# Second mixer of a two-block transformer: a head's output step cut into pieces that stand before later projections' weight loads

## The chip, the cores and the metric

The kernel runs on one core of a Trainium2 chip. The metric is the device time of one execution in microseconds. The times before are 2347.97, 2349.81 and 2349.92 us, median 2349.81 us. A profiled execution of its own stands beside them.

## The reference, cut to what matters

Two transformer blocks over 512 tokens of width 1024, in float32. The first block has a feed-forward part, a mixer of windowed and sparse attention, and a second feed-forward part. The second block has a hybrid mixer and a mixture of 32 experts. The change lies in the hybrid mixer only:

```python
def _hybrid_mixer(u, ...):
    proj = u @ w_in
    gq, gk, gv, gg, gdown, rq, rk, rv, rg, mga, mgb = jnp.split(proj, splits, axis=-1)
    log_a = log_sigmoid(gdown @ gk_up + gk_bias) / 16          # decay, per token and key column
    o_gla = gla(heads(gq * 128 ** -0.5), heads(gk), heads(gv), heads(log_a))       # 4 heads, 128 -> 256
    o_gla = _rmsnorm(o_gla, gla_norm_w) * silu(gg)
    o_ret = retention(rotary(rq), rotary(rk) * 256 ** -0.5, heads(rv))             # 4 heads, 256 -> 512
    o_ret = _group_norm(o_ret, ret_norm_w) * silu(rg)
    y_a, y_b = o_gla @ w_br_gla, o_ret @ w_br_ret
    return (sigmoid(mga) * y_a + sigmoid(mgb) * y_b) @ w_out
```

In the gated linear attention (GLA) a score of query i and key j is a sum over 128 columns of q, k and exp(cum_i - cum_j), where cum is the running sum of the decay. In the retention the score of q and k is multiplied by a fixed power of the distance.

## The kernel before, in words

Activations stand feature-major: a tile is 128 features by 512 tokens. Each float32 matrix product is made of three matmuls with operands split into a high and a low part (`mm3`, lines 99 to 101). For each 512 KB block of weights `load_w` issues one DMA on SP's queue into `wraw` (3 buffers), copies the high part on ScalarE into `whi` (line 84) and takes the low part on VectorE into `wlo` (line 85); `whi` and `wlo` have two buffers each, so that the weights of one projection are split while the one before is multiplied. `gemm` then runs 8 x 3 matmuls of 512 columns.

The second mixer (`mixer2`, line 1000) goes through these steps:

- `gla_decay`: decay sums for all 4 heads.
- GLA, head by head: projections q, k (`gla_qk`) and two gates (`silu_tile`: projection, sigmoid by ScalarE, product on GpSimd); for heads 0 and 2 the values of two heads (`vproj`); then `gla_core`, which builds the 512 x 512 score matrix in ten levels. A level (`level(s)`) makes exp of decay differences and multiplies k and q with them into a tile `gf` (two buffers, VectorE lines 917 and 918); matmuls `gs` follow (lines 927, 933, 950), and their result is split into `sh` and `sl` or put into `sd` by mask. The `gs` matmuls have two PSUM banks. The core is a chain between TensorE and VectorE; matmuls of the next head's projections stand between its steps.
- `head_out`: scores times values (`pvo`, three matmuls a piece), copies `o` and squares `osq` on ScalarE, a sum of the squares on GpSimd (line 816), and then a closure `rest`: a matmul with ones (`on`, line 822), two ScalarE functions for the reciprocal root (`hr_ln`, lines 175 and 177), for each of the head's 2 (GLA) or 4 (retention) tiles a GpSimd product gate * hr (line 826), a VectorE product into `o` (line 828), and its split into `fh` and `fl` (lines 84 and 85).
- After four GLA heads, 8 times: a projection with `wma`, its sigmoid, and the branch product `ya` of the 8 `fh`/`fl` tiles with `wbg`.
- Retention, two heads and then the branch product `yb`, twice: per head two projections each for q and k with rotation (`ret_qk`), `vproj`, four gates, `ret_core` (scores `rs`, then `head_out`). Head 2's q is projected before the first `yb` loop, its k after it. Before the second `yb` loop stand 8 projections with `wmb`.

`rest` is held back: `head_out` stores `[wait, rest]` in `self.pend`, each `proj2` counts one down behind its matmuls (`flush(1)`, line 741), and at zero all of `rest` is issued there. `wait` is 3 for GLA (behind the next head's first gate) and 1 for retention (behind the next head's first projection). `flush()` without a number issues it at once.

The text of the kernel is not the order of issue. A planner in the compiler lays out each engine's queue beforehand: the position in the text is a priority, and an instruction whose operands are due by the planner's own estimate of durations is taken before one with a higher priority that is not. On the chip each queue is then worked through in that fixed order.

Of the kernel before, what the change touches and what calls it, by code (L numbers as in the profile page):

```python
# [9 lines left out]
F32 = mybir.dt.float32  # L10
# [29 lines left out]
class Kern:  # L40
# [694 lines left out]
        tp.release()  # L735

    def proj2(self, src):
        w = self.load_w(src)
        ps = self.acc("pj2")
        self.gemm(ps, w, self.X, DT)  # L740
        self.flush(1)
        return ps

    def sigma(self, ps, a=None):
# [49 lines left out]

        return (self.m2.tile([128, 4, 512], F32R, name="sh"), self.m2.tile([128, 4, 512], F32R, name="sl"))

    def head_out(self, V, c0, nt, sh, sl, wname, w0, gates, wait):

        nc = self.nc
        vh, vl = V  # L800
        O = []
        ssum = None
        for t in range(nt):
            po = self.ps.tile([128, 512], F32, name="pvo", tag="tp", bufs=2)
            for j in range(4):
                q = slice(128 * j, 512)
                v = slice(c0 + 128 * t, c0 + 128 * t + 128)
                self.mm3(po[:, q], vh[:, j, v], vl[:, j, v], sh[:, j, q], sl[:, j, q], j == 0, j == 3)
            o = self.m2.tile([128, 512], F32, name="o", bufs=4)
            nc.scalar.activation(o, po, AF.Copy)  # L810
            sq = self.m2.tile([128, 512], F32, name="osq", bufs=2)
            nc.scalar.activation(sq, po, AF.Square)
            if ssum is None:
                ssum = sq
            else:
                nc.gpsimd.tensor_tensor(out=ssum, in0=ssum, in1=sq, op=OP.add)
            O.append(o)
        F = self.F

        def rest():  # L820
            p = self.ps.tile([128, 512], F32, name="on", tag="pv", bufs=1)
            nc.tensor.matmul(p, self.ones, ssum, start=True, stop=True)
            r = self.rstd_from(p, 1.0 / (128 * nt), "hr", None)
            for t in range(nt):
                g = gates[t]
                nc.gpsimd.tensor_tensor(out=g, in0=g, in1=r, op=OP.mult)
                o = O[t]
                nc.vector.scalar_tensor_tensor(o, o, self.vcol(wname, w0 + t), g, op0=OP.mult, op1=OP.mult)
                fh = self.m2f.tile([128, 512], F32R, name="fh", bufs=8)
                fl = self.m2f.tile([128, 512], F32R, name="fl", bufs=8)  # L830
                self.split(o, fh, fl)
                F.append((fh, fl))
        self.pend = [wait, rest]
        self.flush(0)

    def flush(self, n=99):

        if self.pend:
            self.pend[0] -= n
            if self.pend[0] <= 0:  # L840
                f, self.pend = self.pend[1], None
                f()

    def gla_decay(self):

# [33 lines left out]
        nc.vector.tensor_tensor(out=k, in0=self.proj2(A["wg"][:, h, 1]), in1=self.rstd, op=OP.mult)  # L879
        return q, k  # L880

    def gla_core(self, h, q, k, V, gates):

        nc = self.nc
        c = self.cum[h]
        tot = lambda b: c[:, b, 127:128]
        sh, sl = self.s_tiles()
        sd = self.m3.tile([128, 4, 128], F32, name="sd", bufs=1)  # L890
# [30 lines left out]
        def put(src, dst):  # L921
            self.split(src, dst(sh), dst(sl))

        f = level(256)
        p = self.ps.tile([128, 512], F32, name="gs", tag="lg", bufs=2)
        for j in range(2):
            nc.tensor.matmul(p[:, j * 256:j * 256 + 256], f[:, j * 128:j * 128 + 128], f[:, 256:512],
                             start=(j == 0), stop=(j == 1), skip_group_check=True)
        put(p.rearrange("p (j i) -> p j i", j=2), lambda t: t[:, 0:2, 256:512])
        f = level(128)  # L930
        p = self.ps.tile([128, 512], F32, name="gs", tag="lg", bufs=2)
        for n, j in enumerate((0, 2)):
            nc.tensor.matmul(p[:, n * 128:n * 128 + 128], f[:, j * 128:j * 128 + 128],
                             f[:, j * 128 + 128:j * 128 + 256], start=(n == 0), stop=(n == 1),
                             skip_group_check=True)
        for n, j in enumerate((0, 2)):
            put(p[:, n * 128:n * 128 + 128], lambda t: t[:, j, j * 128 + 128:j * 128 + 256])
        for n, s in enumerate((64, 32, 16, 8, 4, 2, 1, 0)):
            a = b = level(s) if s else None
            if not s:  # L940
                a, b = k, q
            p = self.ps.tile([128, 512], F32, name="gs", tag="lg", bufs=2)

            t = s or 128
            up = lambda v: v.rearrange("p (m u t) -> p m u t", u=2, t=s)[:, :, 1] if s else \
                v.rearrange("p (m t) -> p m t", t=t)
            w = 64 if s else 128
            for j in range(4):
                x = slice(j * 128, j * 128 + 128)
                nc.tensor.matmul(p[:, j * w:j * w + w].rearrange("p (m t) -> p m t", t=t), a[:, x], up(b[:, x]),  # L950
                                 start=(j == 0), stop=(j == 3), skip_group_check=True)
            m = up(self.gmask[:, n])
            nc.vector.copy_predicated(
                sd.rearrange("p j (m u t) -> p j m u t", u=2, t=s)[:, :, :, 1] if s else sd.unsqueeze(2),
                m.unsqueeze(1).to_broadcast([128, 4] + list(m.shape[1:])),
                p[:, 0:4 * w].rearrange("p (j m t) -> p j m t", j=4, t=t))
        for j in range(4):
            put(sd[:, j], lambda t: t[:, j, j * 128:j * 128 + 128])
        self.head_out(V, 256 * (h % 2), 2, sh, sl, "gla_norm", 0, gates, 3)

    def ret_qk(self, h, which):

# [20 lines left out]

    def ret_core(self, h, Q, K, V, gates):
        nc, A = self.nc, self.A
        dec = self.m3.tile([128, 512], F32, name="dec", bufs=1)
        nc.sync.dma_start(dec, A["decay"][:, h])
        sh, sl = self.s_tiles()
        for j in range(4):
            p = self.ps.tile([128, 512], F32, name="rs", tag="lg", bufs=2)  # L990
            q = slice(128 * j, 512)
            x = slice(128 * j, 128 * j + 128)
            for e in range(2):
                self.mm3(p[:, q], K[e][0][:, x], K[e][1][:, x], Q[e][0][:, q], Q[e][1][:, q], e == 0, e == 1)
            s = self.m3.tile([128, 512], F32, name="rsc", bufs=2)
            nc.vector.tensor_tensor(out=s[:, q], in0=p[:, q], in1=dec[:, 0:512 - 128 * j], op=OP.mult)
            self.split(s[:, q], sh[:, j, q], sl[:, j, q])
        self.head_out(V, 0, 4, sh, sl, "ret_norm", 4 * h, gates, 1)

    def mixer2(self):  # L1000
        nc, A = self.nc, self.A
# [5 lines left out]
        nc.sync.dma_start(self.gmask, A["gmask"])  # L1007
        ma = self.dram.tile([128, DT, 512], F32, name="ma")
        yb = self.dram.tile([128, DT, 512], F32, name="yb")
        self.pend = None  # L1010
        self.gla_decay()
        self.F = []
        V = None
        for h in range(4):
            if h == 0:
                V = self.vproj(A["wgv"][:, h // 2], False)
            q, k = self.gla_qk(h)
            gates = [self.silu_tile(A["wg"][:, h, 2 + t]) for t in range(2)]
            if h == 2:
                V = self.vproj(A["wgv"][:, h // 2], False)  # L1020
            self.gla_core(h, q, k, V, gates)
        for n in range(DT):
            _, s = self.sigma(self.proj2(A["wma"][:, n]))
            self.flush()
            w = self.load_w(A["wbg"][:, n])
            po = self.acc("ya")
            self.gemm(po, w, self.F, DT)
            t = self.m2.tile([128, 512], F32, name="mt", tag="gate", bufs=4)
# [6 lines left out]
        for c in (0, 1):  # L1035
            nc.vector.tensor_tensor(out=self.cs[:, c], in0=self.cs[:, c], in1=self.rstd, op=OP.mult)
        M = []
        Q = None
        for half in range(2):
            F = self.F = []  # L1040
            for h in (2 * half, 2 * half + 1):
                Q = Q or self.ret_qk(h, 0)
                K = self.ret_qk(h, 1)
                V = self.vproj(A["wrv"][:, h], True)
                gates = [self.silu_tile(A["wr"][:, h, 4 + t]) for t in range(4)]
                self.ret_core(h, Q, K, V, gates)
                Q = None
            if half == 0:
                Q = self.ret_qk(2, 0)
            if half == 1:  # L1050
                m3.release()
                sp = self.pool("sig")
# [1 line left out]
                for n in range(DT):  # L1054
                    _, g = self.sigma(self.proj2(A["wmb"][:, n]), sp.tile([128, 512], F32, name=f"sg{n}"))
                    sg.append(g)
            self.flush()
            for n in range(DT):
                w = self.load_w(A["wbr"][:, half, n])
                po = self.acc("yb")  # L1060
                self.gemm(po, w, self.F, DT)
                t = self.m2.tile([128, 512], F32, name="mt", tag="gate", bufs=4)
# [10 lines left out]
                h = self.xp.tile([128, 512], F32R, name=f"oh{n}", tag=f"xh{n}")  # L1073
# [9 lines left out]
        for n in range(DT):  # L1083
            w = self.load_w(A["wo2"][:, n])
# [710 lines left out]
```

## Time and profile before

| | |
|---|---|
| median of three runs | 2349.81 us |
| profiled execution, its own time | 2345.84 us |
| span of its trace | 2344.0 us |
| TensorE busy | 2272.5 us, 97% |
| VectorE busy | 1151.0 us, 49% |
| ScalarE busy | 856.7 us, 37% |
| GpSimd busy | 402.7 us, 17% |
| second mixer, in the trace | about 1020 to 1810 us |

The table is one execution's. Busy TensorE is time with a matmul in flight; a wait of TensorE is read from the view of waits, and a lowered clock from the granted clock of a stretch. In the second mixer a projection of 24 matmuls takes about 5.4 us.

### The profile page before, as it was taken

To read this page: it belongs to the slowest core of one execution; us is meant where nothing else is said; L and a number is where in the kernel's file an instruction comes from. 1 tells how busy PE (TensorE), PEld (TensorE's weight loads), DVE (VectorE), ACT (ScalarE), POOL (GpSimd) and SP (SyncE) were. 2 spreads that over 40 slices of the span, in tenths; PEclk is the share of its full clock that TensorE was granted. 3 is DMA by queue.
4 is the path that set the end of the run, shared out by engine and by line. 5 is a ranking of instruction groups with operands and counts; after the bars stand their busy time and mean duration, and the time that the engine had idled before them with its cause. 6 is when DMAs were issued, how large, how long until landed. Compare 5 with 4: busy or idle time off the path is not lost.

```text
span 2344.0 us, 27722 instructions
## 1 busy us (share of the span) xinstructions
PE 2272.5 (97%) x10344; PEld 1674.3 (71%) x10344; DVE 1151.0 (49%) x2074; ACT 856.7 (37%) x1441; POOL 402.7 (17%) x408
## 2 busy tenths in 40 slices
PE   8999999999999999999999999999999899999997
PEld 6888888776788888877877887787878544444443
DVE  4544445888754444457674445435464333322223
ACT  5322234676642222344444354334553211100012
POOL 1000003335310000014340121203123211111001
PEclk9999999999999999999999999999999899999999
DMA  5533335221133333332213322232247999999997
GB/s 168 172 94 93 104 100 162 84 61 50 45 113 99 91 98 99 117 118 63 72 60 111 106 83 83 88 113 69 89 125 229 363 398 407 406 407 406 406 408 304
DMA packets 126098, 390.83 MB, mean 167 GB/s; under 512 B 15398, under 2 KB 21071, under 8 KB 125704
## 3 DMA queue, kind: packets, MB, share of 16 engines
q1 hardware_dynamic: 121064, 380.10, 47.3%
q10 hardware_dynamic: 2592, 4.72, 0.5%
q0 software_dynamic: 2304, 4.20, 0.5%
q8 instruction: 83, 1.36, 0.2%
q14 instruction: 55, 0.45, 0.1%
HBM read 378.44 MB, written 17.33 MB: 169 GB/s over the span
## 4 chain that ended last, share of the span: by engine, by line
PE 87%; DVE 5%; DMA 3%; ACT 3%; POOL 1%; issue 1%; SPq 0%; POOLq 0%; DVEq 0%; ACTq 0%
PE pg L1339 5%; PE pj L101 5%; PE pj L99 5%; PE pj L100 5%; PE pu L1339 5%; PE po L100 4%; PE po L101 4%; PE po L99 4%; PE pd L1339 4%; PE pu L101 3%; PE pu L99 3%; PE pu L100 3%; PE pg L100 3%; PE pg L101 3%; PE pg L99 3%; PE py L1406 2%
## 5 line engine op out<-in xcount | busy, mean ns | idle before, releaser
L84 ACT ACTIVATE whi<-wraw 128x1024 fp32r<-128x1024 f32 (+2 forms) x290 | 296.2, 1021 | 702.0 <-issue 186.8
L85 DVE TENSOR_TENSOR wlo<-wraw,whi 128x1024 fp32r<-128x1024 f32 (+2 forms) x282 | 347.3, 1232 | 141.2 <-ACT whi L84 135.3
L101 PE MATMUL pj<-xh,wlo 128*128 128x512 f32 x624 | 247.4, 397 | 10.3 <-DVE wlo L85 10.3
L99 PE MATMUL pj<-xh,whi 128*128 128x512 f32 x624 | 250.7, 402 | 0.0
L100 PE MATMUL pj<-xl,whi 128*128 128x512 f32 x624 | 246.1, 394 | 0.0
L157 POOL TENSOR_TENSOR ssq<-ssq,sq 128x512 f32<-128x512 f32 x34 | 53.3, 1566 | 762.4 <-ACT sq L154 761.9
L1339 PE MATMUL pg<-wexp,xs 128*64 128x512 f32 x474 | 163.6, 606 | 2.0 <-DMA wexp<-in_wexp 2.0
L1339 PE MATMUL pu<-wexp,xs 128*64 128x512 f32 x474 | 159.8, 592 | 0.0
L99 PE MATMUL pg<-xh,whi 128*128 128x512 f32 x352 | 139.1, 395 | 6.7 <-ACT xh L142 6.7
L101 PEld LDWEIGHTS pj<-xh,wlo 128*128 128x128 f32 x624 | 118.5, 190 | 36.2 <-DVE wlo L85 12.0
L100 PE MATMUL pg<-xl,whi 128*128 128x512 f32 x352 | 138.4, 393 | 0.5 <-DVE xl L143 0.5
L101 PE MATMUL pg<-xh,wlo 128*128 128x512 f32 x352 | 138.1, 392 | 0.0
L101 PE MATMUL pu<-xh,wlo 128*128 128x512 f32 x352 | 137.1, 389 | 0.4 <-DVE wlo L85 0.4
L100 PE MATMUL po<-hl,whi 128*128 128x512 f32 x352 | 137.1, 389 | 0.0
L99 PE MATMUL pu<-xh,whi 128*128 128x512 f32 x352 | 137.1, 389 | 0.0
L99 PE MATMUL po<-hh,whi 128*128 128x512 f32 x352 | 137.0, 389 | 0.0
L100 PE MATMUL pu<-xl,whi 128*128 128x512 f32 x352 | 136.9, 389 | 0.0
L101 PE MATMUL po<-hh,wlo 128*128 128x512 f32 x352 | 136.9, 389 | 0.0
L99 PEld LDWEIGHTS pj<-xh,whi 128*128 128x128 f32 x624 | 118.8, 190 | 25.4 <-issue 2.6
L100 PEld LDWEIGHTS pj<-xl,whi 128*128 128x128 f32 x624 | 118.5, 190 | 24.5 <-issue 1.7
L1339 PE MATMUL pd<-wexp,hs 128*64 128x512 f32 x484 | 115.7, 599 | 0.0
L1339 PEld LDWEIGHTS pu<-wexp,xs 128*64 128x64 f32 x474 | 49.1, 137 | 77.7 <-issue 77.6
(613 smaller groups left out, 4413.3 us busy)
## 6 DMA issues: line engine op xcount, KB each, us to landing
wexp<-in_wexp SPq DMA_DIRECT2D x358, 512.0 KB
wraw<-in_w1i SPq DMA_DIRECT2D x44, 512.0 KB
wraw<-in_w2i SPq DMA_DIRECT2D x44, 512.0 KB
wraw<-in_wr SPq DMA_DIRECT2D x32, 512.0 KB
wpark<-in_wexp SPq DMA_DIRECT2D x48, 256.0 KB
wraw<-in_wg SPq DMA_DIRECT2D x16, 512.0 KB
wraw<-in_wrv SPq DMA_DIRECT2D x16, 512.0 KB
wraw<-in_wbr SPq DMA_DIRECT2D x16, 512.0 KB
```

Of the source, the lines that this page charges most:

```text
L84: return (self.nc.scalar.activation(hi, src, AF.Copy), (eng or self.nc.vector).tensor_tensor(out=lo, in0=src, in1=hi.bitcast(F32), op=OP.s ...
L85: (eng or self.nc.vector).tensor_tensor(out=lo, in0=src, in1=hi.bitcast(F32), op=OP.subtract))
L99: mm(ps, ah, bh, start=first, stop=False)
L100: mm(ps, ah, bl, start=False, stop=False)
L101: mm(ps, al, bh, start=False, stop=last)
L157: self.nc.gpsimd.tensor_tensor(out=self.ssq, in0=self.ssq, in1=sq, op=OP.add)
L1339: self.pe(self.nc.tensor.matmul(out[r], x[:, r], self.loaded[2 * p + j, c][half], start=first, stop=last))
L1406: self.pe(nc.tensor.matmul(ps, oh[:, i * 128:i * 128 + 128], y[:, hf * 512:hf * 512 + 512], start=(first and j == 0), stop=(j == 1)))
```

## The change

It touches the second mixer alone.

- `flush(n)` now takes a list of steps and issues the first n of them. `proj2` calls `flush(1)` ahead of its `load_w`, not behind its matmuls.
- `rest` is cut: `scale` (the matmul `on`, the reciprocal root, all GpSimd products of gates) and `parts(a)` (the VectorE products, `fh` and `fl` of two tiles). The list is: nothing, `scale`, nothing, `parts(0)`, and for retention `parts(2)`. So `scale` stands before the second projection's weights, `parts(0)` before the fourth's, `parts(2)` before the fifth's, for both kinds of heads; the parameter `wait` is gone.
- In GLA the values of the two highest levels (`level(256)`, `level(128)`) are issued between the two gates' projections; the rest of the core is a closure called after the second gate.
- The k of retention head 2 is projected before the first `yb` loop, right behind its q.

```diff
     def proj2(self, src):
+        self.flush(1)
         w = self.load_w(src)
         ps = self.acc("pj2")
         self.gemm(ps, w, self.X, DT)
-        self.flush(1)
         return ps
...
-        def rest():
+        def scale():
             p = self.ps.tile([128, 512], F32, name="on", tag="pv", bufs=1)
             nc.tensor.matmul(p, self.ones, ssum, start=True, stop=True)
             r = self.rstd_from(p, 1.0 / (128 * nt), "hr", None)
-            for t in range(nt):
-                g = gates[t]
+            for g in gates:
                 nc.gpsimd.tensor_tensor(out=g, in0=g, in1=r, op=OP.mult)
-                o = O[t]
+
+        def parts(a):
+            for t in (a, a + 1):
+                g, o = gates[t], O[t]
                 nc.vector.scalar_tensor_tensor(o, o, self.vcol(wname, w0 + t), g, op0=OP.mult, op1=OP.mult)
...
                 self.split(o, fh, fl)
                 F.append((fh, fl))
-        self.pend = [wait, rest]
-        self.flush(0)
+        wait = [lambda: None]
+        self.pend = wait + [scale] + wait + [lambda a=a: parts(a) for a in range(0, nt, 2)]
 
     def flush(self, n=99):
 
-        if self.pend:
-            self.pend[0] -= n
-            if self.pend[0] <= 0:
-                f, self.pend = self.pend[1], None
-                f()
+        for _ in range(min(n, len(self.pend))):
+            self.pend.pop(0)()
...
-        f = level(256)
...
-        f = level(128)
...
+        f, f2 = level(256), level(128)
+
+        def core(V, gates):
+            nonlocal f
...
+            f = f2
...
+            self.head_out(V, 256 * (h % 2), 2, sh, sl, "gla_norm", 0, gates)
+        return core
...
             q, k = self.gla_qk(h)
-            gates = [self.silu_tile(A["wg"][:, h, 2 + t]) for t in range(2)]
+            gates = [self.silu_tile(A["wg"][:, h, 2])]
+            core = self.gla_core(h, q, k)
+            gates.append(self.silu_tile(A["wg"][:, h, 3]))
             if h == 2:
                 V = self.vproj(A["wgv"][:, h // 2], False)
-            self.gla_core(h, q, k, V, gates)
+            core(V, gates)
...
-                K = self.ret_qk(h, 1)
+                K = K or self.ret_qk(h, 1)
...
-                Q = None
+                Q = K = None
             if half == 0:
-                Q = self.ret_qk(2, 0)
+                Q, K = self.ret_qk(2, 0), self.ret_qk(2, 1)
```

## Rows read from the trace of the kernel before

**Rows 1.** The page's busy time of the engines, with shares of the span.
```profile
PE 2272.5 (97%) x10344; PEld 1674.3 (71%) x10344; DVE 1151.0 (49%) x2074; ACT 856.7 (37%) x1441; POOL 402.7 (17%) x408
```
**Rows 2.** Waits of TensorE, 1040 to 1800 us: who for whom, total us, times, longest.
```profile
PE pj L101 <- DVE wlo L85: 10.3, 3, 3.8
PE gs L950 <- DVE sl L85: 6.7, 2, 3.6
PE ya L99 <- ACT fh L84: 1.8, 1, 1.8
PE yb L100 <- DVE fl L85: 1.5, 2, 1.3
...
PE on L822 <- POOL osq L816: 0.7, 1, 0.7
```
**Rows 3.** Stretches: length, busy PE PEld DVE ACT POOL, granted clock, DMA.
```profile
1104.00:1118.00 14.00, 10.87 (x51) 8.95 (x49) 12.15 (x19) 7.06 (x14) 8.36 (x8) 0.88 0.09 32
1203.00:1217.00 14.00, 10.43 (x50) 8.79 (x49) 11.89 (x18) 7.41 (x14) 8.68 (x8) 0.88 0.11 36
1394.00:1426.00 32.00, 28.20 (x113) 22.41 (x112) 21.26 (x22) 10.22 (x14) 13.17 (x10) 0.89 0.17 50
1478.00:1512.00 34.00, 31.23 (x123) 24.05 (x123) 18.35 (x18) 11.62 (x17) 11.48 (x8) 0.90 0.21 64
1604.00:1640.00 36.00, 32.20 (x141) 26.21 (x141) 21.50 (x22) 12.46 (x18) 16.25 (x11) 0.95 0.16 45
1688.00:1718.00 30.00, 27.28 (x125) 22.30 (x125) 17.00 (x19) 18.23 (x29) 10.25 (x7) 1.00 0.30 88
...
1114.00:1116.00 2.00, 2.00 (x9) 1.75 (x8) 1.26 (x2) 1.59 (x4) 0.85 (x2) 0.50 0.00 0
```
**Rows 4.** Timeline of VectorE, GLA heads 0 to 1: start, us, instruction, count.
```profile
1095.70 1.22 DVE L85 TENSOR_TENSOR wlo<-wraw,whi 128x1024 fp32r<-128x1024 f32 x1
1096.83 0.84 DVE L917 TENSOR_TENSOR gf<-gk,gd__9220 128x256 f32<-128x256 f32 x1
...
1105.33 3.48 DVE L828 SCALAR_TENSOR_TENSOR o<-o,vec,gate 128x512 f32<-128x512 f32 x2
1108.74 1.47 DVE L85 TENSOR_TENSOR fl<-o,fh 128x512 fp32r<-128x512 f32 x2
...
1111.39 0.88 DVE L85 TENSOR_TENSOR sl<-gs,sh 128x512 fp32r<-128x512 f32 x2
```
**Rows 5.** Timelines of GpSimd and of TensorE, the same stretch.
```profile
1094.14 1.30 POOL L816 TENSOR_TENSOR osq<-osq 128x512 f32<-128x512 f32 x1 [3.50 <-ACT osq L812]
...
1103.57 2.99 POOL L826 TENSOR_TENSOR gate<-gate,hr_ln 128x512 f32<-128x512 f32 x2 [3.83 <-ACT hr_ln L177]
...
1099.88 1.02 PE L822 MATMUL on<-osq,ones 128*128 128x512 f32 x2
```
**Rows 6.** Timeline of SP's queue, while the first `ya` product is under way.
```profile
1228.34 0.33 SPq L1034 DMA_DIRECT2D csr<-csd  x1
```
**Rows 7.** Timeline of VectorE, retention heads 0 to 1.
```profile
1402.93 5.17 DVE L828 SCALAR_TENSOR_TENSOR o<-o,vec,gate 128x512 f32<-128x512 f32 x3 [1.19 <-POOL gate L826]
1408.02 1.88 DVE L85 TENSOR_TENSOR fl<-o,fh 128x512 fp32r<-128x512 f32 x3
1409.83 0.74 DVE L828 SCALAR_TENSOR_TENSOR o<-o,vec,gate 128x512 f32<-128x512 f32 x1
1410.49 1.27 DVE L971 TENSOR_TENSOR rt<-pj,csr 128x512 f32<-128x512 f32 x2
1411.69 1.37 DVE L85 TENSOR_TENSOR fl<-o,fh 128x512 fp32r<-128x512 f32 x1
1412.98 2.28 DVE L85 TENSOR_TENSOR wlo<-wraw,whi 128x1024 fp32r<-128x1024 f32 x1
```
**Rows 8.** Timelines of GpSimd and of ScalarE, the same stretch.
```profile
1401.60 5.95 POOL L826 TENSOR_TENSOR gate<-gate,hr_ln 128x512 f32<-128x512 f32 x4 [4.74 <-ACT hr_ln L177]
...
1408.67 1.05 ACT L84 ACTIVATE whi<-wraw 128x1024 fp32r<-128x1024 f32 x1
```

More of the change, by code (lines that the diff above doesn't have):

```diff
@@ L795, in s_tiles, with head_out @@
         return (self.m2.tile([128, 4, 512], F32R, name="sh"), self.m2.tile([128, 4, 512], F32R, name="sl"))
-    def head_out(self, V, c0, nt, sh, sl, wname, w0, gates, wait):
+    def head_out(self, V, c0, nt, sh, sl, wname, w0, gates):
         nc = self.nc
@@ L880, in gla_qk, with gla_core @@
         return q, k
-    def gla_core(self, h, q, k, V, gates):
+    def gla_core(self, h, q, k):
         nc = self.nc
@@ L922, in put @@
             self.split(src, dst(sh), dst(sl))
-        f = level(256)
[L925 to L929, printed above, removed]
-        f = level(128)
-        p = self.ps.tile([128, 512], F32, name="gs", tag="lg", bufs=2)
@@ L932, in gla_core @@
[L932 to L941, printed above, removed]
-            p = self.ps.tile([128, 512], F32, name="gs", tag="lg", bufs=2)
[L944 to L947, printed above, removed]
-            for j in range(4):
[L949 to L956, printed above, removed]
@@ L957, in gla_core @@
-        for j in range(4):
-            put(sd[:, j], lambda t: t[:, j, j * 128:j * 128 + 128])
-        self.head_out(V, 256 * (h % 2), 2, sh, sl, "gla_norm", 0, gates, 3)
+        f, f2 = level(256), level(128)
+        def core(V, gates):
+            nonlocal f
+            p = self.ps.tile([128, 512], F32, name="gs", tag="lg", bufs=2)
+            for j in range(2):
+                nc.tensor.matmul(p[:, j * 256:j * 256 + 256], f[:, j * 128:j * 128 + 128], f[:, 256:512],
+                                 start=(j == 0), stop=(j == 1), skip_group_check=True)
+            put(p.rearrange("p (j i) -> p j i", j=2), lambda t: t[:, 0:2, 256:512])
+            f = f2
+            p = self.ps.tile([128, 512], F32, name="gs", tag="lg", bufs=2)
+            for n, j in enumerate((0, 2)):
+                nc.tensor.matmul(p[:, n * 128:n * 128 + 128], f[:, j * 128:j * 128 + 128],
+                                 f[:, j * 128 + 128:j * 128 + 256], start=(n == 0), stop=(n == 1),
+                                 skip_group_check=True)
+            for n, j in enumerate((0, 2)):
+                put(p[:, n * 128:n * 128 + 128], lambda t: t[:, j, j * 128 + 128:j * 128 + 256])
+            for n, s in enumerate((64, 32, 16, 8, 4, 2, 1, 0)):
+                a = b = level(s) if s else None
+                if not s:
+                    a, b = k, q
+                p = self.ps.tile([128, 512], F32, name="gs", tag="lg", bufs=2)
+                t = s or 128
+                up = lambda v: v.rearrange("p (m u t) -> p m u t", u=2, t=s)[:, :, 1] if s else \
+                    v.rearrange("p (m t) -> p m t", t=t)
+                w = 64 if s else 128
+                for j in range(4):
+                    x = slice(j * 128, j * 128 + 128)
+                    nc.tensor.matmul(p[:, j * w:j * w + w].rearrange("p (m t) -> p m t", t=t), a[:, x], up(b[:, x]),
+                                     start=(j == 0), stop=(j == 3), skip_group_check=True)
+                m = up(self.gmask[:, n])
+                nc.vector.copy_predicated(
+                    sd.rearrange("p j (m u t) -> p j m u t", u=2, t=s)[:, :, :, 1] if s else sd.unsqueeze(2),
+                    m.unsqueeze(1).to_broadcast([128, 4] + list(m.shape[1:])),
+                    p[:, 0:4 * w].rearrange("p (j m t) -> p j m t", j=4, t=t))
+            for j in range(4):
+                put(sd[:, j], lambda t: t[:, j, j * 128:j * 128 + 128])
+            self.head_out(V, 256 * (h % 2), 2, sh, sl, "gla_norm", 0, gates)
@@ L997, in ret_core @@
             self.split(s[:, q], sh[:, j, q], sl[:, j, q])
-        self.head_out(V, 0, 4, sh, sl, "ret_norm", 4 * h, gates, 1)
+        self.head_out(V, 0, 4, sh, sl, "ret_norm", 4 * h, gates)
     def mixer2(self):
@@ L1009, in mixer2 @@
         yb = self.dram.tile([128, DT, 512], F32, name="yb")
-        self.pend = None
+        self.pend = []
         self.gla_decay()
@@ L1046, in mixer2 @@
                 self.ret_core(h, Q, K, V, gates)
-                Q = None
+                Q = K = None
             if half == 0:
-                Q = self.ret_qk(2, 0)
+                Q, K = self.ret_qk(2, 0), self.ret_qk(2, 1)
             if half == 1:
```

## The prediction

> **What bounds the kernel now.** The page comes first: TensorE is busy for 2272.5 us, 97% of the span, and the next, VectorE, for 49% [rows 1]. So a change that adds no matmul and removes none can only win back TensorE's idle time and the time in which it ran slowly. The view of its waits says where that is in the second mixer [rows 2]: 10.3 us in three waits of a projection for the low part of its weights (`wlo`), 6.7 us in two waits of a GLA core for a split score tile (`sl`), 1.8 us of `ya` for `fh`, and waits of `yb` for `fl` and its like. The windows around them give each stall its idle time (length less busy PE) and the clock [rows 3]: idle 3.1, 3.6, 3.8, 2.8, 3.8 and 2.7 us. All six lie just behind the output of a head: A and B at GLA heads 1 and 3, D and F at retention heads 1 and 3, E where `yb` follows head 1, G where the `wmb` projections follow head 3. After five of them TensorE runs for some microseconds at the lower of its two levels, 1.2 GHz (the row with 0.50 shows two of A's). A window's length times (1 - clock) bounds what that costs: 1.7, 1.7, 3.5, 3.4, 1.8 and 0 us. Idle 19.8 and clock 12.1 make 31.9 us, the ceiling.
>
> The timelines say why. In A, VectorE had its two `o` products from 1105.33 to 1108.81 and their `fl` until 1110.2, and only then reached the core's `sl`, which TensorE stood waiting for until 1112.2 [rows 2, 4]. The `o` products came so late because `on` ran at 1099.88, behind the first gate's projection, and the GpSimd products only from 1103.57 [rows 5], though the sum of squares was there at 1095.44 [rows 5]. In D the whole output of four tiles goes through at once: three `o` beside the GpSimd products (5.17 us), `fl`, the fourth `o`, rotation, the last `fl`, and then the fourth projection's `wlo`, which ends at 1415.26 [rows 7]. Its `whi` on ScalarE waited from the same cause, behind the third `fh` [rows 8].
>
> **The change, part by part.** *`scale` earlier in GLA* (3 places: heads 0 to 1, 1 to 2, 2 to 3). `on` no longer has to stand behind k's and the gate's projections; its only condition is the sum, at 1095.44. So it comes 4.4 us earlier (1099.9 - 1095.5), and with it everything behind: the last `fl` ends at 1105.8 in place of 1110.2. The core's first `sl` could then run as soon as its scores are there, and stalls of 3.1 and 3.6 us go, with their 1.7 us of clock each. What is late next is the sum itself: the one `on` that was issued straight behind its sum cost TensorE 0.7 us of waiting [rows 2]; I charge that at all three places. Saved: A 3.1 + 1.7 - 0.7 = 4.1, B 3.6 + 1.7 - 0.7 = 4.6, heads 1 to 2 (no such stall, since `vproj` lies between) -0.7.
>
> *`parts` in two pieces in retention.* `on` keeps its place, behind the first projection. The queues are laid out beforehand and what is due is taken early: the load of `csr`, whose text stands behind eight `ya` products, is issued at 1228.34, during the first [rows 6]. So a piece whose gates are ready is taken when VectorE is free, wherever its text stands, and only what still competes with the rotation and `wlo` at the end gives way. That is the last `o` and its `fl`, 0.74 + 1.37 = 2.1 us [rows 7]. `wlo` ends 2.1 us earlier, and of 3.8 us in D and F 1.7 remain. The bounds are 0 saved (the planner's order stays as it is) and 3.8 (the third tile gives way too, and `whi` with it). I take the middle because the row shows the fourth `o` already separated from the first three. Half of the clock's share is kept as a cost. D: 3.8 + 3.5 - 1.7 - 1.7 = 3.9; F: 3.8 + 1.8 - 1.7 - 0.9 = 3.0; G, the same with a sigmoid in the rotation's place: 2.7 - 0.6 = 2.1.
>
> *Head 2's k before `yb`.* Two more projections (10.8 us) now lie between `on` and the first `yb`; the last `fl` has long been there. E's 2.8 + 3.4 us go. But the boundary now has the form of D, four projections behind a head, and gets D's remainder, 1.7 + 1.7. Saved: 2.7. The projections themselves are moved, with their 512 KB loads on SP's queue, by one loop; their cover does not change, because the next head's values follow directly in both forms.
>
> *Levels 256 and 128 between the gates.* Their `gf` were already made early: one of the four halves stands at 1096.83 in VectorE's queue, ahead of `on` and of the second gate's projection [rows 4, 5], and the `gs` matmuls keep their place behind that projection. Costed at nothing; the gates' projections cover them, and without that cover they are at most 4 x 0.84 = 3.4 us of VectorE per head.
>
> *GpSimd's products moved by 4.4 us in GLA* fall beside a `wlo`. A `wlo` took 1.22 us alone and 2.28 beside GpSimd's rotation [rows 4, 7], and an `o` 0.74 alone against 1.7 beside the gate products [rows 7]. The `wlo` concerned is that of the next head's q, needed only after the second gate's projection, so TensorE does not see the 1.1 us. The Trainium skill, "SBUF — State Buffer", section "Who interferes with whom", speaks against this part: a VectorE instruction with two SBUF inputs and a GpSimd instruction that reads SBUF exclude each other for a whole instruction. The durations agree; were the three `wlo` on the path, that would take 3 x 1.1 = 3.3 us off the sum below, 16.4.
>
> The sum: 4.1 + 4.6 - 0.7 + 3.9 + 3.0 + 2.1 + 2.7 = 19.7 us. The `ya` wait of 1.8 us stays: `flush()` still issues head 3's output whole at that place. The profiled execution took 2345.84 us and would take 2326.1; the median of the runs lies 4.0 higher, so 2349.8 - 19.7 = 2330.1. I say 2330. The experts behind the mixer start their loads from its last loop and shift with it.
>
> **The rivals.** *1: all of it goes.* If the second piece really leaves the queue until it is wanted, D, E, F and G lose all idle and clock. 31.9 less three `on` waits (2.1) is 29.8: 2320. For it: VectorE is under half busy [rows 1]. Against: GpSimd takes 1.49 us per product in a row of four [rows 8], whoever waits for them.
>
> *2: the pieces are taken as early as before.* Then D, F and G stay, and E becomes a second D (3.8 + 3.5 in place of 2.8 + 3.4, 1.1 worse). Only GLA's 8.0 is left: 6.9 us, 2343. For it: rows 6, and a VectorE with nothing else due when the gates come.
>
> *3: slower, the `o` products get ahead of the second gate's weights in GLA.* `parts(0)` now precedes that `load_w` in the text. VectorE works in order: if its queue has the two `o` before that `wlo` (at 1095.70 today, rows 4), `wlo` waits for GpSimd. The pair of `o` would end at 1108.8 - 4.4 = 1104.4, `wlo` at 1105.6, and TensorE wants it at about 1100.8, as the gate's projection begins right behind `on` [rows 5]: 4.8 us of idling and some 2.6 of clock, three times, 22.2 us. With rival 2's retention the whole is 22.2 - 6.9 = 15.3 us slower, 2365; with my terms for retention 2352. It decides once the planner thinks the first gate ready before that `wlo`. On the chip the distance is from 1095.70 to 1095.5 + 3.7 = 1099.2 (from `on` to the gates, rows 5), 3.5 us, which speaks against it.
>
> *4: nothing happens.* The planner lays the same queues, because text position is only a priority: 2349.8.
>
> **How the numbers follow.** My forecast 0.45, rival 1 0.17, rival 2 0.19, rival 3 0.09, rival 4 0.10. The range 2318 to 2348 holds nearly all of the forecast with its bounds, rivals 1 and 2 in the main, and leaves out rival 3 and most of 4. A measurement of this kernel tells about 0.2%, 4.7 us, from no change: faster is below 2345.1 (0.43 + 0.17 + 0.14 from rival 2), slower above 2354.5 (0.06 from rival 3, 0.01 from 4), the rest is the same: 0.74, 0.19, 0.07.
>
> **What would show it.** In the profile after: `on` of GLA heads right behind the sum of squares, and no wait of `gs` for `sl` of 3 us; waits of `pj` for `wlo` shrunk to some 1.7 us each but four of them (D, the new one before `yb`, F, a small G); no wait of `yb` for `fl`; the granted clock at 1.00 around A and B. I am wrong if a new wait of `pj` for `wlo` stands at a GLA head's second gate (rival 3), if D's wait is still 3.8 us (rival 2), or if it is gone (rival 1).

## The result, and the profile after

The kernel after takes 2334.6 us (median of 4 runs, 2332.75 to 2335.86) beside 2349.59 us before on the same chip: ratio 0.994, 95% interval 0.9928 to 0.9952, by the medians 15.0 us less. The forecast was 2330, 19.7 us less.

The two profiled executions differ by 10.0 us only (2345.84 and 2335.86 us): the one of before lay below its median, and in the one of after the unchanged code ahead of the mixer took 2.8 us longer. So two stages are compared inside the traces: "GLA" from the first `pz` matmul (the decay's first) to the last of `ya`, "retention" from the first `rs` to the last of `yb` (starts of matmuls, from the views of these tiles).

| us | before | after | change | forecast |
|---|---|---|---|---|
| GLA | 294.0 | 292.3 | -1.7 | -8.0 |
| retention | 400.6 | 387.8 | -12.8 | -11.7 |
| first `pz` to last `yb` | 760.1 | 745.6 | -14.5 | -19.7 |

So the total hides a miss: retention gave slightly more than its sum, GLA next to nothing.

The page of the kernel after, busy time of the engines (it answers to [rows 1]):

```profile
PE 2266.3 (97%) x10344; PEld 1669.1 (72%) x10344; DVE 1149.6 (49%) x2074; ACT 858.3 (37%) x1441; POOL 400.6 (17%) x408
```

The waits of TensorE in the kernel after, 1020 to 1820 us (they answer to [rows 2]; us in total, times, longest):

```profile
PE pj L101 <- DVE wlo L85: 8.0, 5, 2.6
PE gs L952 <- DVE gf L917: 3.5, 5, 1.5
PE on L822 <- POOL osq L816: 3.3, 4, 1.4
PE ya L99 <- ACT fh L84: 1.8, 1, 1.8
PE vv L100 <- DVE wlo L85: 1.1, 2, 0.5
PE ya L101 <- DVE wlo L85: 0.4, 1, 0.4
PE yb L101 <- DVE wlo L85: 0.3, 1, 0.3
```

The 6.7 us of `gs` for `sl` are gone, and so are the waits of `yb` for `fl` and `fh`. In their place stand waits of `gs` for `gf`, of `on` for the sum and of `pj` for `wlo`. The timeline of TensorE has them one by one (start, us, instruction; in brackets the idle time before it and what ended it):

```profile
1098.25 1.12 PE L822 MATMUL on<-osq,ones 128*128 128x512 f32 x2 [0.64 <-POOL osq L816]
...
1116.27 0.52 PE L952 MATMUL gs<-gf 128*128 128x64 f32 x3 [1.47 <-DVE gf L917]
...
1195.44 0.70 PE L822 MATMUL on<-osq,ones 128*128 128x512 f32 x1 [1.40 <-POOL osq L816]
...
1206.25 0.51 PE L101 MATMUL pj<-xh,wlo 128*128 128x512 f32 x1 [2.61 <-DVE wlo L85]
...
1414.17 0.50 PE L101 MATMUL pj<-xh,wlo 128*128 128x512 f32 x1 [1.50 <-DVE wlo L85]
...
1495.25 0.50 PE L101 MATMUL pj<-xh,wlo 128*128 128x512 f32 x1 [1.49 <-DVE wlo L85]
...
1619.65 0.50 PE L101 MATMUL pj<-xh,wlo 128*128 128x512 f32 x1 [1.50 <-DVE wlo L85]
...
1700.12 0.50 PE L101 MATMUL pj<-xh,wlo 128*128 128x512 f32 x1 [0.86 <-DVE wlo L85]
```

The last four are D, the new boundary ahead of `yb`, F and G: the forecast had 1.7, 1.7, 1.7 and 0.6. The fourth row, at the second gate of GLA head 3, is the wait that rival 3 described. VectorE's timeline shows both (first the GLA gate, then D, which answers to [rows 7]):

```profile
1203.52 1.10 DVE L830 SCALAR_TENSOR_TENSOR o<-o,vec,gate 128x512 f32<-128x512 f32 x1
1204.54 1.66 DVE L85 TENSOR_TENSOR wlo<-wraw,whi 128x1024 fp32r<-128x1024 f32 x1
...
1404.08 5.17 DVE L830 SCALAR_TENSOR_TENSOR o<-o,vec,gate 128x512 f32<-128x512 f32 x3 [1.19 <-POOL gate L825]
1409.18 1.88 DVE L85 TENSOR_TENSOR fl<-o,fh 128x512 fp32r<-128x512 f32 x3
1410.99 1.27 DVE L974 TENSOR_TENSOR rt<-pj,csr 128x512 f32<-128x512 f32 x2
1412.19 1.93 DVE L85 TENSOR_TENSOR wlo<-wraw,whi 128x1024 fp32r<-128x1024 f32 x1
1414.04 1.77 DVE L830 SCALAR_TENSOR_TENSOR o<-o,vec,gate 128x512 f32<-128x512 f32 x1
```

In D exactly the fourth `o` and its `fl` have moved behind `wlo`; the first three stay ahead of it, though the text puts the third behind it. In GLA head 3 an `o` stands ahead of the second gate's `wlo`, which ends at 1206.20, and TensorE starts at 1206.25.

### The profile page after: what moved, and what is told of

It reads as the page before. It is cut to its first block, busy times and chain, and to the rows that moved or that the text cites. A ratio compares the mean times of both kernels' runs of the same rounds, so it can differ in the third digit from the quotient of the medians.

```text
span 2334.1 us, 27726 instructions
## 1 busy us (share of the span) xinstructions
PE 2266.3 (97%) x10344; PEld 1669.1 (72%) x10344; DVE 1149.6 (49%) x2074; ACT 858.3 (37%) x1441; POOL 400.6 (17%) x408
## 4 chain that ended last, share of the span: by engine, by line
PE 84%; DVE 5%; DMA 4%; ACT 3%; POOL 2%; issue 1%; SPq 0%; POOLq 0%; DVEq 0%; ACTq 0%
PE pg L1344 6%; PE pu L1344 5%; PE pj L101 4%; PE pj L100 4%; PE pj L99 4%; PE po L100 4%; PE po L101 4%; PE po L99 4%; PE pd L1344 4%; PE pu L101 3%; PE pu L100 3%; PE pu L99 3%; PE pg L101 3%; PE pg L100 3%; PE pg L99 3%; PE py L1411 2%
```

## The experiments

The first two rows are the result above. The other runs were timed beside the kernel before on the same chip, in four batches (e1 to e4; c1 and e5 to e7; e9, e11 and e12; e13), in which the median of before was 2346.69, 2347.01, 2348.7 and 2348.16 us. "Ret." is the retention stage; the waits are those of TensorE in the GLA stage, from 1020 us on; the last column bounds the time lost there to a lowered clock, first between 1020 and 1040 us, then from 1040 us on, worked out from windows of 10 us as length x (1 - granted clock). The stages, waits and clocks are those of one profiled execution of each run, which for e11 and e12 was its fastest.

| run | us | ratio, 95% interval | GLA | ret. | GLA waits | GLA clock |
|---|---|---|---|---|---|---|
| before | 2349.59 | | 294.0 | 400.6 | 10.0 | 3.4 + 5.1 |
| after | 2334.6 | 0.994 [0.9928, 0.9952] | 292.3 | 387.8 | 11.6 | 3.4 + 0 |
| c1, after again | 2334.14 | 0.9947 [0.9933, 0.996] | 292.9 | 387.8 | 11.1 | 0 + 5.1 |
| e1, GLA half only | 2347.01 | 1.0 [0.9991, 1.0009] | 292.4 | 399.5 | 11.7 | 3.5 + 0 |
| e2, retention half only | 2334.44 | 0.9948 [0.9934, 0.9962] | 294.0 | 387.7 | 10.0 | 3.5 + 5.1 |
| e3, k late | 2338.81 | 0.9966 [0.9952, 0.9979] | 292.4 | 392.6 | 11.6 | 3.4 + 0 |
| e4, levels back | 2338.73 | 0.9966 [0.9952, 0.9979] | 295.7 | 387.7 | 11.8 | 1.7 + 6.8 |
| e5, sum on VectorE | 2335.78 | 0.995 [0.9937, 0.9964] | 294.6 | 387.8 | 10.0 | 3.4 + 5.1 |
| e6, retention pieces behind | 2335.52 | 0.9954 [0.994, 0.9967] | 292.9 | 387.4 | 11.1 | 1.7 + 3.4 |
| e7, GLA pieces behind | 2336.3 | 0.9952 [0.9938, 0.9965] | 295.0 | 387.8 | 10.9 | 3.4 + 5.1 |
| e9, second `fl` on GpSimd | 2340.97 | 0.9966 [0.9952, 0.998] | 292.9 | 394.2 | 11.2 | 1.7 + 3.4 |
| e11, gate product early, on after | 2323.98 | 0.9898 [0.9883, 0.9913] | 290.2 | 378.9 | 11.2 | 0 + 1.7 |
| e12, the same, on before | 2317.74 | 0.9872 [0.9857, 0.9887] | 283.6 | 378.9 | 6.9 | 0 + 0 |
| e13, e11 with GLA's output late | 2320.33 | 0.9883 [0.9864, 0.9902] | 285.7 | 378.9 | 7.8 | 1.7 + 0 |

Take the waits and both parts of the clock off the GLA stage and 275.4 to 277.4 us are left in all fourteen rows. So what differs between the rows is waits and clock, and up to 8.6 us of it is clock, which differs between executions of one program too (after and c1).

### Each half alone: e1 and e2

e1 keeps the GLA half and puts retention's output back to `rest` as it was, head 2's k behind `yb`; e2 is its mirror (`nt == 2` held back behind three projections, the levels back in the core). The diff is e1's.

```diff
+        def whole():
+            scale()
+            for a in range(0, nt, 2):
+                parts(a)
+        if nt == 4:
+            self.behind_mm = [1, whole]
+        else:
+            self.pend = wait + [scale] + wait + [lambda a=a: parts(a) for a in range(0, nt, 2)]
...
-                Q, K = self.ret_qk(2, 0), self.ret_qk(2, 1)
+                Q = self.ret_qk(2, 0)
```

> Only the GLA half of the change: scale and parts as steps ahead of the weight loads and the two levels between the gates for GLA heads; retention heads issue their whole output behind the first projection, and head 2's k stands behind the yb loop, both as before. Theory A (from the stages of the two traces: GLA gave about 2 us, retention 14): 2 to 4 us faster than before, ratio 0.998 to 0.999. Theory B (the split that was predicted: GLA 8.0 us): 2341.6, ratio 0.9966. In the trace both expect the retention stalls of 3.8 us at heads 1 and 3 back, with the clock falling there.

> Only the retention half: steps ahead of the loads for retention heads and head 2's k ahead of yb; GLA heads issue their whole output behind the third projection, and the two levels are back in the core. Theory A: 12 to 15 us faster than before, ratio 0.9936 to 0.9949, nearly the whole of the change. Theory B: 11.7 us, ratio 0.995, and clearly short of the changed kernel. Both expect the two waits of gs for sl of 3.1 and 3.6 us back, with the clock falling behind them.

e1 measured 1.0 [0.9991, 1.0009], so GLA's half is worth nothing within 2.1 us, which refutes theory B (8.0 us) and leaves only the low end of theory A; e2 has the whole gain (0.9948). The GLA waits say why: 10.0 us before, 11.7 in e1. The `sl` waits (6.7) went, and `on` (0.7 to 3.4), `gf` (0.8 to 3.5) and `wlo` (0 to 2.6) took their place.

### Parts of the change undone: e3 and e4

e3 takes head 2's k behind the `yb` loop again; e4 puts the two levels back into the core.

```diff
-                Q, K = self.ret_qk(2, 0), self.ret_qk(2, 1)
+                Q = self.ret_qk(2, 0)
```

```diff
-        f, f2 = level(256), level(128)
...
-            nonlocal f
+            f = level(256)
...
-            f = f2
+            f = level(128)
```

> The changed kernel, but head 2's k is projected behind the first yb loop again. Theory A: the yb stall of before comes back (2.8 us idle and up to 3.4 us of clock) in place of 1.8 us of waits for wlo, so 3 to 4.4 us slower than the changed kernel: 0.995 to 0.996 of before. Rival: the pieces are taken early anyhow, the position of k is worth nothing, and the time is the changed kernel's, 0.994.

> The changed kernel, but levels 256 and 128 are issued in the core, behind the second gate, as before. Theory A: no difference from the changed kernel beyond 1 us (0.994), and the wait of 2.6 us for wlo at GLA head 3's second gate stays, since the o products and the sum of squares stand before that wlo. Rival: the levels' VectorE work is what holds that wlo up; without it the wait shrinks below 1 us and the kernel is 2 us faster than the changed one (0.993).

e3: of retention's 12.8 us, 8.0 remain (400.6 to 392.6); k early is worth the other 4.8, not 2.7. The waits of TensorE in e3, 1380 to 1790 us:

```profile
PE yb L99 <- ACT fh L84: 4.4, 1, 4.4
PE pj L101 <- DVE wlo L85: 3.8, 3, 1.5
```

With the pieces cut and k late, `yb` waits longer than before (4.4 us against 2.8 of idle time at E in [rows 3]), and the granted clock behind that is 0.68 over 10 us. The cut alone makes E worse; k early is what makes it safe.

e4 is 4.3 us slower than e2 of the same batch by the medians; the intervals just overlap, but the five executions of e4 (2337.99 to 2340.26 us) all lie above the five of e2 (2333.75 to 2337.79). It is also 4.6 us slower than c1 of another batch. Neither theory had that: the wait for `wlo` at head 3 went, as the rival said, and the time rose. e4 and e2 differ in the early `scale` and `parts` of GLA alone, so e4 against e2 is that step by itself: a loss of some 4 us, which the early levels make up for. The waits are hardly longer than after (11.8 us), but gathered: `gs` waits 6.4 us for `gf` in three places, the longest 3.1. The clock lost 6.8 us there. In the two traces the way from the first `pz` to the last `yb` differs by 1.7 us only (748.9 and 747.2), so one execution of each doesn't show the whole 4.3. e13, below, has the levels early and GLA's output late, and its stage is within 2.1 us of that of e12, which has both late; 1.7 of these are clock at the start of the stage. So the place of the levels seems to matter only beside the early scale; the runs go no further.

### Other orders of the same work: c1, e5, e6, e7

c1 is the kernel after, run again. e5 makes GLA's sum of squares on VectorE. e6 orders retention's `parts(2)` on VectorE behind the low part of the fourth projection's weights, where the text has it anyhow, so that it can't be taken early; e7 orders GLA's `parts(0)` behind the low part of the second gate's weights, which the text puts it ahead of.

```diff
-                nc.gpsimd.tensor_tensor(out=ssum, in0=ssum, in1=sq, op=OP.add)
+                (nc.vector if nt == 2 else nc.gpsimd).tensor_tensor(out=ssum, in0=ssum, in1=sq, op=OP.add)
```

```diff
+        if self.pend and self.pend[0][0]:
+            self.pend.pop(0)[1](self.last_lo)
...
+                if after is not None:
+                    self.behind(ins, after)
```

> The changed kernel once more, on the same chip as the three above, so that they can be compared with it: 12 to 17 us faster than before, ratio 0.993 to 0.995.

> The changed kernel with the sum of a GLA head's squares on VectorE in place of GpSimd. Theory A: TensorE's 3.3 us of waiting for that sum in front of the matmul with ones are a cost of the early scale step, since the planner takes GpSimd's add for shorter than its 1.3 us; with the sum on VectorE (about 0.7 us) the waits fall below 1 us in all, and the kernel is 2 to 3 us faster than the changed one. Rival: the core behind it is a chain that starts no sooner, the idle time turns up in the waits of gs for gf, and the time is the changed kernel's within 1 us.

> The changed kernel with the second two tiles of a retention head's output ordered behind the low part of the fourth projection's weights on VectorE, by a dependency, so that they can't be taken early. Theory A (the third tile in front of that weight's split, on VectorE and ScalarE, makes the remaining waits of 1.5 us): the waits of pj for wlo at retention heads fall from 5.3 us in all below 1 us, and the kernel is 4 to 5 us faster than the changed one, 0.992 of before. Rival: the work only moves behind, in front of the next weights, whose waits (now 1.1 us at the values, 0.3 at yb) grow by as much; the time stays within 1 us.

> The changed kernel with a GLA head's output products ordered behind the low part of the second gate's weights. This moves instructions at the boundary of GLA heads 2 to 3 alone. Theory A: the wait of 2.6 us for that wlo goes, and with it 2 to 3 us of time. Rival: the products come back into the core's start, the wait of gs for gf behind it grows, and less than 1 us is left.

None of them is faster than c1. In e5 the waits for the sum fall from 3.3 us to 0.6, and the longest wait for `gf` rises from 1.5 to 2.8; all GLA waits together are 10.0 us, 1.1 less than c1's, and the time is not. In e7 the 2.6 us at the second gate of head 3 are gone; its waits, 1020 to 1820 us, have them here:

```profile
PE gs L960 <- DVE gf L925: 5.7, 5, 2.8
```

In e6 the retention waits for `wlo` of `pj` fall from 5.3 us to 1.1. Its waits, 1380 to 1790 us:

```profile
PE vv L100 <- DVE wlo L85: 3.6, 2, 1.8
PE yb L101 <- DVE wlo L85: 1.6, 1, 1.6
PE pj L101 <- DVE wlo L85: 1.1, 4, 0.3
```

That is 6.3 us beside 6.7 after. So the rivals had the mechanism in all three: where one wait goes, the next one grows, and the sum of a stage's waits falls by at most 1.1 us beside c1. (The medians lie 1.4 to 2.2 us above c1's, which the intervals don't tell from no difference.) That suggests that TensorE waits less for a place in the queue than for the amount of VectorE's and GpSimd's work between a head's last scores and the next thing that TensorE needs. It is not shown in general: k early and, below, e13 against e11 change nothing but the order, and their stages are 4.8 and 4.5 us shorter.

### Less work for VectorE: e9

The last two tiles' `fl` go to GpSimd.

```diff
-                self.split(o, fh, fl)
+                self.split(o, fh, fl, nc.gpsimd if a == 2 else None)
```

> The changed kernel with the low part of the second two tiles of a retention head's output (two of the subtractions into fl) on GpSimd in place of VectorE. Theory C (after the ordering runs: at a retention boundary VectorE's own work, slowed beside GpSimd, is what TensorE's idle time is made of): taking 2 x 0.7 us off VectorE shrinks the waits of pj, vv and yb at the four boundaries by about 1 us each, 2 to 4 us in all. Rival: GpSimd's subtraction excludes VectorE for as long as it saved, and delays the rotation's products on GpSimd; the time stays within 1 us or grows.

Retention is 6.4 us slower than after (394.2). The waits of `pj` for `wlo` there rise from 5.3 to 9.3 us, and up to 5.1 us of clock are lost. The timelines of GpSimd and then of VectorE in e9, at D:

```profile
1408.57 1.61 POOL L85 TENSOR_TENSOR fl<-o,fh 128x512 fp32r<-128x512 f32 x1 [1.29 <-ACT fh L84]
1411.41 1.26 POOL L978 TENSOR_TENSOR rt<-rt 128x512 f32<-128x512 f32 x1 [1.23 <-DVE rt L974]
1412.63 2.27 POOL L85 TENSOR_TENSOR fl<-o,fh 128x512 fp32r<-128x512 f32 x1
1414.86 1.28 POOL L977 TENSOR_TENSOR rt<-rt 128x512 f32<-128x512 f32 x1
```

```profile
1407.75 1.28 DVE L85 TENSOR_TENSOR fl<-o,fh 128x512 fp32r<-128x512 f32 x2
1408.95 1.78 DVE L830 SCALAR_TENSOR_TENSOR o<-o,vec,gate 128x512 f32<-128x512 f32 x1
1410.66 1.27 DVE L974 TENSOR_TENSOR rt<-pj,csr 128x512 f32<-128x512 f32 x2
1411.85 1.90 DVE L85 TENSOR_TENSOR wlo<-wraw,whi 128x1024 fp32r<-128x1024 f32 x1
```

An `fl` takes 1.29 to 2.27 us on GpSimd, against 0.69 on VectorE, and the rotation stands behind it. But no matmul waits for the rotation; what TensorE waits for is `wlo`, and that comes later because VectorE's queue has another order: the fourth `o`, which stood behind `wlo` after, now stands ahead of it, with 1.78 us in place of the third `fl`'s 0.6. At D, at the new boundary and at F the wait rises from 1.5 to 2.6 us. So e9 doesn't test less work on VectorE with the rest of the order kept.

### The product that makes the chain long: e11, e12, e13

In both kernels GpSimd's gate * `hr_ln` can only start when the reciprocal root is there, and VectorE's `o` runs beside it. The product of three factors can be taken in another order: gate * o on GpSimd as soon as `o` is copied out, before `on`, and then norm weight * `hr_ln` times that on VectorE. e11 does this in the kernel after, e12 in the kernel before with nothing of the change. The same function is computed, with the factors in another order.

```diff
+        for g, o in zip(gates, O):
+            nc.gpsimd.tensor_tensor(out=g, in0=g, in1=o, op=OP.mult)
...
-                nc.gpsimd.tensor_tensor(out=g, in0=g, in1=r, op=OP.mult)
...
-                nc.vector.scalar_tensor_tensor(o, o, self.vcol(wname, w0 + t), g, op0=OP.mult, op1=OP.mult)
+                nc.vector.scalar_tensor_tensor(o, g, self.vcol(wname, w0 + t), r, op0=OP.mult, op1=OP.mult)
```

> The changed kernel with the product taken in another order: GpSimd multiplies gate by the head's output right behind the copies, ahead of the matmul with ones, and VectorE multiplies by the norm's weight and hr_ln behind it; GpSimd has nothing to do any more between hr_ln and the products. The number of instructions is the same. Theory C (the chain hr_ln, GpSimd product, VectorE product beside it is what makes a boundary last): a product on VectorE takes 0.74 in place of 1.7 us and none waits for GpSimd; at D, E and F the waits of 1.5 us and those of vv and yb behind them go, at GLA head 3 the 2.6 us; 5 to 9 us faster than the changed kernel, 0.991 to 0.993 of before. Rival (idle time that goes at one place comes back at the next, as in the three ordering runs): within 2 us of the changed kernel.

> The kernel before with the same other order of the product and nothing of the change: the whole output is still issued at once. Theory C: without the GpSimd products behind hr_ln the burst on VectorE is 4 x 0.74 + 4 x 0.7 in place of about 10 us, D, F and G lose most of their 3.8, 3.8 and 2.7 us and A and B theirs; 12 to 20 us faster than before, about as fast as the changed kernel or faster. Rival: the order in the text, steps ahead of the loads, is what counts, and this gains less than 5 us.

Both beat the kernel after, and e12, without the change, is the fastest of all: 31.0 us below before by the medians. Both gained more than was expected (the ratios were to be 0.991 to 0.993, and 12 to 20 us): of the 32.1 us between the first `pz` and the last `yb` that e12's trace has less than that of before, 16.1 are waits (23.0 to 6.9), and the rest is in the main lost clock: the windows of before lose up to 17.0 us there, those of e12 none. The rows of the `o` products by line (shortest, median and longest in ns), first of after, then of e12:

```profile
L830 DVE SCALAR_TENSOR_TENSOR o<-o,vec,gate x24: 737/1769/1791, 1103.6 to 1701.2; 128x512 f32<-128x512 f32 x24
```

```profile
L829 DVE SCALAR_TENSOR_TENSOR o<-gate,vec,hr_ln x24: 743/747/751, 1101.5 to 1674.4; 128x512 f32<-128x512 f32 x24
```

The timeline of VectorE in e12, D's place:

```profile
1390.85 2.07 DVE L829 SCALAR_TENSOR_TENSOR o<-gate,vec,hr_ln 128x512 f32<-128x512 f32 x3
1392.84 1.89 DVE L85 TENSOR_TENSOR fl<-o,fh 128x512 fp32r<-128x512 f32 x3
1394.64 0.75 DVE L829 SCALAR_TENSOR_TENSOR o<-gate,vec,hr_ln 128x512 f32<-128x512 f32 x1
```

Three `o` take 2.07 us, not 5.17, and start right behind a `wlo` without 1.19 us of waiting for a gate: 4.3 us less on VectorE's queue at each of these places, more than D's whole stall of 3.8. Two things went together here, the slowing of VectorE's products beside GpSimd's and the wait for a GpSimd product between `hr_ln` and `o`; no run has one without the other. All waits of the retention stage are gone (none of `pj`, `vv` or `yb` is left between 1380 and 1790 us), and it takes 378.9 us with or without the change.

With the products out of the way the GLA half costs time: the stage takes 290.2 us in e11, 283.6 in e12, and the four executions of e11 (2321.54 to 2326.73 us) all lie above those of e12 (2314.77 to 2321.0). e13 takes e11 and puts GLA's whole output ahead of the fourth weight again, levels left early.

```diff
+        if nt == 2:
+            self.pend = wait * 3 + [lambda: (scale(), parts(0))]
```

> The changed kernel with the product gate times head output ahead of the reciprocal root (as in the run of the changed kernel with that order, 0.990 of the time before), but in GLA the scale and both tiles' parts stand together ahead of the fourth weight, where the kernel before had them; the two levels stay between the gates. Theory: in GLA the early scale is what costs the 6.6 us of stage time that the same order took less on the kernel before (290.2 against 283.6 us from the first head's gate to the last ya): on then stands behind a sum that GpSimd makes after the gate products, 6.7 us of waits. Put late, those waits fall to about 2 us, the stage takes 284 us and the whole about 2317 to 2319 us, ratio 0.987. Rival: the levels between the gates, or the retention half, cost it: the waits for the sum fall, others rise, and it stays at about 2324 us, ratio 0.990, stage 289 us or more.

The stage falls to 285.7 us, near the theory's 284 and not the rival's 289 or more; the total, 2320.33 us, lies 1.3 above the theory's range. By the total alone e11 and e13 are not apart, since their intervals overlap. The waits for the sum, 1020 to 1820 us, first of e11, then of e13:

```profile
PE on L825 <- POOL osq L816: 6.7, 4, 2.2
```

```profile
PE on L825 <- POOL osq L816: 1.8, 1, 1.8
```

An early `on` waits for the sum at every GLA head, since GpSimd makes the sum behind two gate products; an `on` three projections later finds it there.

## Why the prediction was right, and where it was not

**Retention's terms held.** The step by which only the last `o` and its `fl` give way came out as written: these two moved, and D and F wait 1.5 us where the sum said 1.7, G 0.86 where it said 0.6. By the waits the stage lost 6.3 us of idle time (13.0 to 6.7), and the sum had 7.4: the new boundary ahead of `yb` also left 0.3 at `yb` and 1.1 at `vv`. What was mis-sized is "Half of the clock's share is kept as a cost": none was. The granted clock is 1.00 in every window of 10 us between 1380 and 1790 after, and in c1; before, those windows lose 8.5 us. (Idle time and clock, 6.3 + 8.5, make more than the 12.8 us that the stage lost: a window's lost clock is a bound.) So k early was worth 4.8, not 2.7, in the main because the D-like form left its 1.5 us but none of the clock charged to it. That 12.8 lies so near 11.7 is in part luck: too much idle time and too little clock were taken off, and the two errors have opposite signs.

**GLA's term of 8.0 failed, at two steps.** Its measure is 0 within 2.1 us (e1), and by the text's own sign (a new wait of `pj` for `wlo` at a GLA head's second gate) it was wrong there. The chain did start earlier: `on` runs at 1098.25, right behind a sum that GpSimd ended at 1098.20, where before it stood 4.4 us behind [rows 5]; and no `gs` waits for `sl`. The first step that failed is "stalls of 3.1 and 3.6 us go", taken as time won but for the sum. They went and were replaced. Only the `on` waits were charged, at 0.7 each or 2.1 in all, and they rose by 2.6; not charged were `gf` (+2.7), `wlo` at head 3 (+2.6) and `wlo` at `ya` (+0.4). Sum of idle time: -6.7 + 8.3 = 1.6 us more than before. "What is late next is the sum itself" named one of four. The question of what is late next was answered by the next instruction in line, but VectorE, GpSimd and ScalarE had the same work to do in the same stretch, as e5 and e7 show, where removing one wait lengthens another.

The second is "with their 1.7 us of clock each". In the trace of after the clock is back at all places; in c1, the same program, it is not. The windows of after, then of c1 (columns as in [rows 3], the clock being the number before the DMA share):

```profile
1020.00:1040.00 20.00, 20.00 (x69) 13.62 (x68) 13.61 (x27) 10.79 (x18) 1.49 (x2) 0.83 0.17 58
1110.00:1120.00 10.00, 8.53 (x50) 7.02 (x49) 8.32 (x16) 5.33 (x11) 5.03 (x6) 1.00 0.35 105
1200.00:1210.00 10.00, 7.39 (x33) 5.77 (x32) 8.97 (x11) 5.27 (x8) 4.15 (x5) 1.00 0.21 58
1240.00:1250.00 10.00, 7.78 (x31) 5.11 (x30) 7.92 (x9) 5.51 (x8) 2.34 (x2) 1.00 0.20 47
```

```profile
1020.00:1040.00 20.00, 19.62 (x77) 13.85 (x76) 15.45 (x38) 11.60 (x20) 1.49 (x2) 1.00 0.18 52
1110.00:1120.00 10.00, 8.58 (x51) 7.86 (x51) 8.89 (x19) 4.03 (x7) 7.16 (x9) 0.83 0.18 53
1200.00:1210.00 10.00, 8.03 (x31) 6.65 (x32) 6.09 (x8) 6.08 (x9) 2.12 (x2) 0.83 0.36 107
1240.00:1250.00 10.00, 9.23 (x31) 6.59 (x32) 6.32 (x9) 5.61 (x8) 0.00 (x0) 0.83 0.41 130
```

After lost 3.4 us of clock at the start of the stage, in code that the change doesn't touch, and none later; c1 lost none at the start and 5.1 later. Their stages are 0.6 us apart. A gain of clock read from one execution is thus no gain of the kernel: with stalls still there at other places, it may fall there or not.

**The levels, "Costed at nothing".** e4 speaks against it by some 4 us. So the early `scale`, for which 8.0 us were forecast, by itself lost about as much as the levels won back.

**Rival 3** had the mechanism right and the place too wide: it happens at one head of three, for 2.6 us and not 4.8. The text put the deciding distance at 3.5 us for heads 0 to 1, and there it held. **Rival 2** is refuted by e2 and the D rows, **rival 1** by the remaining 1.5 us (it was right in that retention's clock came back whole), **rival 4** by the result.

**What the text had in hand and didn't price.** It read an `o` at 1.7 us beside the gate products and 0.74 alone [rows 7], and used it only to ask whether the moved products would slow a `wlo`. That cost stood in the middle of the chain in both kernels, and so did the wait for the gate product itself; removing both is worth twice the change (31.0 us beside 15.0). At D before, three `o` and three gate products went through in 5.17 us [rows 7, 8]; one after the other they would take 3 x 0.74 + 3 x 1.29 = 6.1 us (1.29 is a gate product in e12). The Trainium skill, "SBUF — State Buffer", section "Who interferes with whom", says that a VectorE instruction with two SBUF inputs and a GpSimd instruction that reads SBUF exclude each other for a whole instruction. The trace agrees but for some 0.3 us a pair.

One reading there is wrong: the `wlo` of 1.22 us at 1095.70 [rows 4] was not alone. The figure holds, since the `wlo` at 1101.38 took 1.23 us with GpSimd idle, but the row also shows who can pay. GpSimd's rows before, in that stretch:

```profile
1095.86 1.53 POOL L913 TENSOR_TENSOR gd__9248<-cum 128x256 f32<-128x256 f32 x1 [0.41 <-DVE gf L917]
...
1098.52 0.62 POOL L913 TENSOR_TENSOR gd__9261<-cum 128x256 f32<-128x256 f32 x1 [0.36 <-DVE gf L918]
```

Here VectorE had begun first and lost nothing, and GpSimd took 1.53 us for what it does in 0.62.

## What to carry to other kernels

Where TensorE waits for a chain of other engines, taking a step of it earlier can only move the idle time to the chain's next link, as GLA did here, unless work leaves the stretch; so list all waits of the stage after the move, not only the one that goes. Shorten the chain before reordering it: look for a factor that needn't wait for the late scalar, and take that product before. Don't book a clock that comes back in one execution as won: in GLA it fell at three places or at none in executions of the same program, while in retention it stayed at 1.00 in after, c1 and e2 alike, with waits of 1.5 us left.

## What the runs showed of the hardware that was not expected

The granted clock of one program differs between its executions: 0.83 at 1110, 1200 and 1240 us in c1 and 1.00 there in after, with waits of up to 2.6 us in both; before, it stayed at 1.00 behind a wait of 2.7 us (G) [rows 3] and fell behind one of 1.8 us (`ya` at 1241.84, 0.83 in 1240 to 1250 us):

```profile
1240.00:1250.00 10.00, 8.19 (x29) 6.21 (x29) 7.39 (x9) 5.62 (x8) 0.57 (x1) 0.83 0.35 105
```

And a subtraction into `fl` that takes VectorE 0.69 us took GpSimd 1.29 to 2.27 us in e9, and slowed the VectorE instruction beside it (the fourth `o`, 1.78 us against 0.74).
